# Layer 0's entry written in another order: modulation steps beside turning products, ctx's squares among x's, single PSUM banks, ropes behind the values

## The chip, the cores and the metric

One core of one Trainium2 chip runs the whole program: two transformer blocks on 512 tokens (x) with a prefix of 256 context tokens (ctx), model width 1024, all in float32 accuracy. The metric is the device time of one execution in microseconds (us); lower is better.

TensorE does the matrix products in "three-pass" form: each float32 operand is split into a rounded high part and a low part (what the rounding left), and three matmuls are added in PSUM (high x high, high x low, low x high). ScalarE (ACT in the profile) makes the high parts, VectorE (DVE) or GpSimd (POOL) the low parts.

## The reference

Only the first mixer of layer 0 matters here, up to its queries, keys and values:

```python
def rmsnorm(x, g):
    y = x * lax.rsqrt(jnp.mean(x * x, axis=-1, keepdims=True) + EPS)
    return y * g
def modulate(x, g, shift, scale):
    return rmsnorm(x, g) * (1 + scale) + shift
mod  = silu(c)     @ ada_w[0] + ada_b[0]      # six parts of 1024: shift, scale, gate, ...
modc = silu(c_ctx) @ ada_w[0] + ada_b[0]
a  = modulate(h,  norm1_g[0], sh1,  sc1)      # x,   512 tokens
ac = modulate(hc, norm1_g[0], csh1, csc1)     # ctx, 256 tokens
u, v, q, k, vv = split(a @ w_in)              # q and k: 512 wide each, vv: 512 wide
q = apply_rope(q, cos, sin); k = apply_rope(k, cos, sin)
kc, vvc = split(ac @ w_in[:, KV_START:])
```

Then come a differential attention over x and ctx, a gated chunk MLP, the output product, a feed-forward part, and layer 1.

## The kernel before, in words

Activations lie with the model width on the 128 partitions: x is eight tiles `hx[k]` (128 x 512), ctx eight tiles `hc[k]` (128 x 256). Everything that the change touches is in `even()`, before the attention. The program is written as straight code. Most steps go through `run(key, ...)` (also as `act`, `dve`, `chain`, `fetch`), which keeps the order in which they are written, engine by engine; steps that do not go through it are placed by a scheduler, which goes by the written order and its own estimate of when a step can start. The engines' queues are in order: an instruction that waits holds everything behind it on its engine.

The stages of the entry, in the times of the profile:

- 8 to 44 us: the scale part of the modulation is made in four quarters. `quarter_steps(q)` runs 32 small matmuls on a slab of `ada_w` (1 MB, loaded on SP's queue) into the one bank of `fill()`; ScalarE copies the row out (`half_row`), `quarter_turn` turns it onto the partitions by a matmul, `quarter_mod` adds bias and gain (VectorE). Then `x_hi(k)`, `x_lo(k)` split x times its scale, and `project(k)` multiplies it with the k-th slice `W[k]` of 4 x 128 columns of q and k weights, adding into four accumulators `accx`. The norm's root is taken out of the product: it is multiplied in at the end. `square(...)` sums x's squares meanwhile: a ScalarE square and a VectorE addition for each k.
- `sums` adds those squares over the partitions (matmuls with ones), takes the root by a chain of ten small VectorE steps (`rsqrt_small`, Newton) and puts it on four diagonal tiles; `spread` turns that into rows (a matmul with ones). rxs and rcs are the rows of x and of ctx.
- 38 to 40 us and 50 to 52 us: `half_steps(0)`, `half_steps(1)`: the shift part, in two halves of 64 small matmuls, turned by `half_turn` and added by `shift_mod`.
- 45 to 62 us: ctx's products with the same eight `W[k]`, 258 columns (256 tokens and two columns with the shift of x and of ctx, whose products are the biases `bc`) into `accc`. `sums(rcs)` stands ahead of k = 4, `spread` ahead of k = 7. `c_hi`, `c_lo` split ctx's operand.
- 62 to 113 us: `ada_four` (part of the later modulation, 16 matmul groups, into `fill()`), then the values: eight k, each one unit of the v weights against six 128-token tiles. The operand `AX_[k]` is made for each k by `normed` (times root and scale) and `shifted` (plus shift, split). Among these steps stand, for every second k, the steps on q and k: times rxs, plus bias, ctx's part times rcs, ScalarE's bias on ctx's part. `rope` follows: a VectorE shuffle into a `tmp("t")` tile (two buffers), a VectorE product with cos, and two GpSimd steps. After k = 4 `ada_four` runs again, ScalarE copies its row into a `tmp("t")` tile (line 465), and after k = 5 `ada_out` turns that row on TensorE.

PSUM has eight banks: three of `bank()`, one of `fill()`, and a pool of four more. Before, the entry uses them as two tiles of two banks (`wide()`), with two accumulators in each.

## Time and profile before

| | |
|---|---|
| median of 3 runs | 1539.58 us (1539.14 to 1540.97) |
| the profiled execution | 1540.77 us, of which 1539.0 us lie between its first and last instruction (the span) |
| mean granted clock of TensorE | 0.993 |
| busy share of the span | TensorE 97%, VectorE 71%, GpSimd 53%, ScalarE 48% |
| moved by DMA | 162.27 MB, 105 GB/s on average |
| TensorE busy from 10 to 100 us | 81.7 of 90 us |

The profile's views used here: the page's first part (busy time), the waits (who waited for whom), the timeline (one instruction a line: start, duration, engine, line of the code, tiles written <- read, sizes, and in brackets the idle time before it and what ended it), and windows (busy time of each engine in a stretch, with the granted clock as a share of full speed). TensorE's matmuls overlap: a 128x512 one is listed with some 0.39 us, but in a run of them one starts every 0.23 us, and a 128x258 one every 0.12 us; what a stage takes is read from starts.

### The profile page before, as it was taken

How to read it: one execution, taken by the hardware profiler on the slowest of the kernel's cores; microseconds unless marked ns; L12 is line 12 of the kernel's file. 1: busy time of each engine (PE TensorE's matmuls, PEld its weight loads, DVE VectorE, ACT ScalarE, POOL GpSimd, SP SyncE). 2: the span in 40 equal slices, each digit the busy share in tenths (PEclk: the TensorE clock that was granted, in tenths of full speed). 3: DMA queues.
4: the chain of work that ended last, by engine and by line, in shares of the span. 5: the costliest groups of instructions: out<-in, count | busy, mean ns of one | idle time of the engine just before them, and what ended most of it. 6: DMA issues, size and time to landing. Idle time of an engine off the chain costs nothing.

```text
span 1539.0 us, 25035 instructions
## 1 busy us (share of the span) xinstructions
PE 1494.3 (97%) x9573; PEld 1345.9 (87%) x9573; DVE 1091.6 (71%) x1941; ACT 738.6 (48%) x1518; POOL 818.7 (53%) x557
## 2 busy tenths in 40 slices
PE   9989999899999999999999999999999999999998
PEld 7758888799999999999999988777879899999997
DVE  4862887766788788888786487676667976666655
ACT  4434666554543333333333354667665554444444
POOL 2352330051266776677776544541323498888882
PEclk9999999999999999999999999999999999999999
DMA  9853100051132332444542211210134232323201
GB/s 353 322 195 126 46 7 1 30 191 54 69 109 98 130 113 101 144 166 143 171 166 75 81 42 57 68 42 15 62 117 165 68 111 97 110 92 115 89 22 56
DMA packets 54504, 162.27 MB, mean 105 GB/s; under 512 B 6256, under 2 KB 8688, under 8 KB 46704
## 3 DMA queue, kind: packets, MB, share of 16 engines
q1 hardware_dynamic: 47328, 135.37, 25.3%
q10 hardware_dynamic: 7056, 25.30, 4.8%
q8 instruction: 75, 1.23, 0.3%
q14 instruction: 45, 0.37, 0.1%
HBM read 158.55 MB, written 2.10 MB: 104 GB/s over the span
## 4 chain that ended last, share of the span: by engine, by line
PE 77%; DVE 11%; ACT 3%; issue 2%; POOL 1%; DMA 0%; DVEq 0%; ACTq 0%; POOLq 0%
PE pw L116 10%; PE pw L115 10%; PE pw L117 10%; PE pb L115 8%; PE pb L116 8%; PE pb L117 8%; PE pf L115 3%; PE pf L116 3%; PE pf L117 3%; PE pb L1943 3%; PE pb L1932 2%; PE pw L1894 1%; DVE t L49 1%; PE pw L1897 1%; PE pf L49 1%
## 5 line engine op out<-in xcount | busy, mean ns | idle before, releaser
L1092 DVE SCALAR_TENSOR_TENSOR xT<-pb,mod,xT 128x512 f32<-128x512 f32 (+3 forms) x204 | 143.2, 708 | 128.4 <-PE pb L117 128.2
L116 PE MATMUL pw<-ax,w 128*128 128x384 f32 (+2 forms) x716 | 227.2, 318 | 3.1 <-DVE ax L49 3.0
L115 PE MATMUL pw<-ax,w 128*128 128x384 f32 (+2 forms) x716 | 226.6, 318 | 3.3 <-DVE q L49 1.9
L117 PE MATMUL pw<-ax,w 128*128 128x384 f32 (+2 forms) x716 | 226.7, 317 | 0.1
L49 POOL TENSOR_TENSOR w<-raw,w 128x512 fp32r<-128x512 f32 x122 | 185.6, 1539 | 47.4 <-ACT w L49 47.2
L92 POOL TENSOR_TENSOR w<-raw,w 128x512 fp32r<-128x512 f32 (+1 forms) x70 | 102.1, 1465 | 197.3 <-ACT w L89 167.1
L49 POOL TENSOR_TENSOR w<-t,w 128x512 fp32r<-128x512 f32 x99 | 149.6, 1515 | 55.6 <-ACT w L49 55.6
L115 PE MATMUL pb<-hh,w 128*128 128x512 f32 x480 | 171.0, 356 | 1.2 <-DVE xT L1092 1.2
L117 PE MATMUL pb<-hh,w 128*128 128x512 f32 x480 | 171.5, 357 | 0.4 <-DVE w L49 0.4
L116 PE MATMUL pb<-hh,w 128*128 128x512 f32 x480 | 171.1, 356 | 0.0
L115 PE MATMUL pw<-T,w 128*128 128x384 f32 (+1 forms) x508 | 156.6, 310 | 2.5 <-DVE hs L1300 1.2
L116 PE MATMUL pw<-T,w 128*128 128x384 f32 (+1 forms) x508 | 157.0, 310 | 1.2 <-DVE T L132 1.2
L117 PE MATMUL pw<-T,w 128*128 128x384 f32 (+1 forms) x508 | 157.0, 310 | 0.0
L115 PE MATMUL pf<-ax,w 128*128 128x256 f32 (+2 forms) x444 | 146.8, 331 | 1.2 <-ACT f L828 0.7
L117 PE MATMUL pf<-ax,w 128*128 128x256 f32 (+2 forms) x444 | 145.7, 328 | 0.0
L116 PE MATMUL pf<-ax,w 128*128 128x256 f32 (+2 forms) x444 | 144.7, 326 | 0.0
L116 PEld LDWEIGHTS pw<-ax,w 128*128 128x128 f32 x716 | 135.9, 190 | 8.4 <-DVE ax L49 4.5
L115 PEld LDWEIGHTS pw<-ax,w 128*128 128x128 f32 x716 | 135.4, 190 | 8.3 <-DVE q L49 2.6
L117 PEld LDWEIGHTS pw<-ax,w 128*128 128x128 f32 x716 | 135.8, 190 | 2.5 <-DVE w L1263 0.4
L49 POOL TENSOR_TENSOR hh<-hs,hh 128x768 fp32r<-128x768 f32 (+1 forms) x42 | 77.9, 1855 | 93.0 <-ACT hh L49 68.8
L49 POOL TENSOR_TENSOR w<-rawo,w 128x512 fp32r<-128x512 f32 x59 | 103.6, 1757 | 28.2 <-ACT w L49 28.2
L240 DVE SCALAR_TENSOR_TENSOR junk<-ar,cb 128x1024 bf16<-128x1024 f32 x64 | 106.8, 1669 | 0.0
(445 smaller groups left out, 3925.0 us busy)
## 6 DMA issues: line engine op xcount, KB each, us to landing
raw<-ffn_in SPq DMA_DIRECT2D x44, 1024.0 KB, 5.4
ar<-ada ACTq DMA_DIRECT2D x48, 512.0 KB, 3.5
rawo<-ffn_out SPq DMA_DIRECT2D x88, 256.0 KB, 2.9
ar<-ada SPq DMA_DIRECT2D x20, 1024.0 KB, 8.4
raw<-odd_out SPq DMA_DIRECT2D x28, 256.0 KB, 2.6
ar<-adas SPq DMA_DIRECT2D x8, 512.0 KB, 7.4
raw<-qk SPq DMA_DIRECT2D x16, 256.0 KB, 5.2
raw<-uv SPq DMA_DIRECT2D x16, 256.0 KB, 2.7
```

The source lines that it names most:

```text
L49: self.tail[key] = fn(*args, **kw)
L92: eng.tensor_tensor(lo, raw, hi.bitcast(F32), ALU.subtract)
L115: mm(out, s[0], m[0], start=start, stop=False, **kw)
L116: mm(out, s[0], m[1], start=False, stop=False, **kw)
L117: return mm(out, s[1], m[0], start=False, stop=stop, **kw)
L240: return self.nc.vector.scalar_tensor_tensor(junk, t, 1.0, self.cb[who], ALU.mult, ALU.mult, accum_out=self.acc[who][:, col:col + 1])
L1092: ins = self.nc.vector.scalar_tensor_tensor(h, ps[:, r], self.modcol(l, j, m, who), h, ALU.mult, ALU.add)
L1894: nc.tensor.matmul(ps[:, st:en], Q, K[g][p][:, b0 * P:b1 * P], start=p == 0, stop=p == 1, skip_group_check=True)
L1897: last = nc.tensor.matmul(ps[:, en:en + TC], Q, K[g][p][:, TX:], start=p == 0 and not edge, stop=p == 1, skip_group_check=True)
L1932: last = nc.tensor.transpose(pt[:, x * P:(x + 1) * P], es[2 * (x % 2) + x // 2][:, kb * P:(kb + 1) * P], self.ident)
L1943: nc.tensor.matmul(po[64 * h:64 * h + 64, :], V[vb][:, 64 * g:64 * g + 64], t[:, h * TC:h * TC + TC], start=kb == 0, stop=kb == nb - 1, sk ...
```

## The change

Nothing is computed otherwise; all of it is order and place. In the words of the code:

1. Loads: the slab of quarters 1 to 3 is fetched ahead of its pair of `W` slices, not behind it.
2. Modulation: `quarter_steps(3)` and `half_steps(0)` move into the middle of `project(3)` and `project(5)`, right behind the turn; `half_steps(1)` from ctx's k = 3 to right behind `project(7)`.
3. `sums` is cut in two. The matmuls over x's squares go into the middle of `project(7)`; the root (`rooted`) follows after the evictions of `accx`, and x's `spread` moves from ahead of ctx's products to ctx's k = 2.
4. ctx's squares 0 to 3 move ahead of `project(7)`, squares 4 to 7 ahead of ctx's products; `c_hi`, `c_lo` of k = 6, 7 go behind `half_steps(1)`'s turn. `sums(rcs)` stays at k = 4; its `spread` moves from k = 7 to k = 6.
5. The accumulators are four tiles of one bank (`single()`); the pool is given back and opened again ahead of the attention. The row of `ada_four` is copied into a `tmp("q")` tile.
6. All steps on q and k and the four ropes move behind the values' code. The bias steps lose their fixed order.

```diff
-        idle = self.wide()
+        idle = self.single()
@@ ada_four
-                row = self.tmp("t")
+                row = self.tmp("q")
                 nc.scalar.copy(row, ps_of.pop(j))
@@ loads
         for k in range(2, KT, 2):
+            slabs[k // 2] = quarter_load(k // 2)
             w_load(k)
             w_load(k + 1)
-            slabs[k // 2] = quarter_load(k // 2)
             x_load(k)
@@
         def sums(acc, T):
-            rd = self.rstd_diag([(acc, T)], 1.0 / D)[0]
-            self.tail["PE"], self.tail["DVE"] = self.last_sum, self.last_diag
-            return rd
+            ps = self.bank()
+            for j in range(T // P):
+                c = slice(j * P, (j + 1) * P)
+                chain(nc.tensor.matmul, ps[:, c], acc[:, c], self.ones, start=j == 0, stop=True, ...)
+            return ps, T // P
+
+        def rooted(ps, n):
+            ms, dg = self.small(n), self.tmp()
+            with tc.issue_after(self.tail["DVE"].ins):
+                nc.vector.tensor_scalar(ms, ps[:, :n * P]..., 1.0 / D, EPS, ALU.mult, ALU.add)
+            rt = self.rsqrt_small(ms, n)
+            for j in range(n):
+                self.tail["DVE"] = nc.vector.tensor_scalar(dg[:, j * P:(j + 1) * P], self.ident, rt[:, j:j + 1], None, ALU.mult)
+            return dg[:, :n * P]
@@ x's products
+        row = quarter_steps(1)
         for q in (1, 2, 3):
             k = 2 * q
-            row = quarter_steps(q)
             got = []
-            project(k - 1, lambda: got.append(quarter_turn(row)))
+            def mid():
+                got.append(quarter_turn(row))
+                if q > 1:
+                    got.append(quarter_steps(3) if q == 2 else half_row(half_steps(0)))
+            project(k - 1, mid)
...
             project(k)
+            row = got[1] if q > 1 else quarter_steps(2)
...
-        row = half_steps(0)
-        with tc.issue_after(self.tail["PE"].ins), tc.issue_after(self.tail["DVE"].ins):
-            rd = sums(rxs, TX)
-        project(7, lambda: got.append(half_turn(row)))
+        c_squares(0, 4)
+        def mid():
+            got.append(half_turn(row))
+            with tc.issue_after(self.tail["PE"].ins):
+                got.append(sums(rxs, TX))
+        project(7, mid)
+        last = half_steps(1)
...
-        rx = spread(rd)
-        act(nc.scalar.copy, rxs, rx)
-        for i in range(2, 8):
-            c_hi(i)
-            c_lo(i)
-        w2 = [self.wide(), self.wide()]
-        accc = [w[:, h * 512:h * 512 + TC + 2] for w in w2 for h in range(2)]
+        rd = rooted(*got[3])
+        c_parts(2, 3)
+        row = half_row(last)
+        c_parts(3, 6)
+        c_squares(4, 8)
+        accc = [self.single()[:, :TC + 2] for _ in range(4)]
         for k in range(KT):
-            if k == 3:
-                row = half_steps(1)
+            if k == 2:
+                pt = half_turn(row)
+                rx = spread(rd)
+                act(nc.scalar.copy, rxs, rx)
+                shift_mod(1, pt)
+                c_parts(6, 8)
             elif k == 4:
-                with tc.issue_after(self.tail["PE"].ins), tc.issue_after(self.tail["DVE"].ins):
-                    rd = sums(rcs, TC)
-            elif k == 7:
+                ms = sums(rcs, TC)
+                rd = rooted(*ms)
+            elif k == 6:
                 rc = spread(rd)
...
@@ the operands of the values: steps on q and k taken out
-            if k % 2:
-                t = qk[keys[k // 2]]
-                dve(nc.vector.tensor_tensor, t[:, :TX], t[:, :TX], rxs, ALU.mult)
-                dve(nc.vector.tensor_scalar, t[:, :TX], t[:, :TX], bc[:, k // 2, 0:1], None, ALU.add)
-                if k // 2 % 2:
-                    dve(nc.vector.tensor_tensor, t[:, TX:], t[:, TX:], rcs, ALU.mult)
-                act(nc.scalar.activation, t[:, TX:], t[:, TX:], AF.Identity, bias=bc[:, k // 2, 1:2])
-        for n in (0, 4, 1, 5):
-            self.rope(qk[n][:, :TX], qk[n][:, :TX], tabs)
@@ behind the values
+        for n in (0, 2, 1, 3):
+            t = qk[keys[n]]
+            dve(nc.vector.tensor_tensor, t[:, :TX], t[:, :TX], rxs, ALU.mult)
+            nc.vector.tensor_scalar(t[:, :TX], t[:, :TX], bc[:, n, 0:1], None, ALU.add)
+            if n % 2:
+                dve(nc.vector.tensor_tensor, t[:, TX:], t[:, TX:], rcs, ALU.mult)
+            nc.scalar.activation(t[:, TX:], t[:, TX:], AF.Identity, bias=bc[:, n, 1:2])
+            self.rope(t[:, :TX], t[:, :TX], tabs)
@@ ahead of the attention
+        self.wp.release()
+        self.open_wide()
```

What that does to the instructions' order is shown at three places. In the rows, pb, pf and pw are PSUM tiles, ax the split operands, f the q and k tiles (f_44 to f_47 before, f_46 to f_49 after), sq the sums of squares, cp ctx's split operand, sm small columns of the root.

VectorE at the end of x's products, before:

```order
L49 TENSOR_TENSOR sq_204<-sq_204,q_457 128x512
L49 SCALAR_TENSOR_TENSOR cp<-hc_38_161,mod_70,cp 128x256 x2
L174 TENSOR_SCALAR sm_499<-pb_500 128x4
L144 TENSOR_SCALAR sm_506<-sm_499 128x4
L146 TENSOR_TENSOR sm_507<-sm_506 128x4
```

And after:

```order
L49 TENSOR_TENSOR sq_206<-sq_206,q_494 128x512
L49 SCALAR_TENSOR_TENSOR cp<-hc_38_161,mod_70,cp 128x256 x2
L49 TENSOR_TENSOR sq_206<-sq_206,q_502 128x256
L49 TENSOR_TENSOR sq_206<-sq_206,t_505 128x256
L49 TENSOR_TENSOR sq_206<-sq_206,q_508 128x256
L49 TENSOR_SCALAR f_48_202<-pw_197 128x512
L49 TENSOR_TENSOR mod_69<-pb_517,adab 128x4
L49 TENSOR_TENSOR mod_70<-pb_517,adab 128x4
L49 TENSOR_TENSOR cp<-mod_69,cp 128x4
L49 TENSOR_TENSOR cp<-mod_70,cp 128x4
L49 TENSOR_SCALAR f_47_201<-pw_198 128x512
L517 TENSOR_SCALAR sm_573<-pb_519 128x4
```

Three additions of ctx's squares and the evictions now stand ahead of x's root, which before came first.

ScalarE in the values' stage, around the copy of `ada_four`'s row (L465), before:

```order
L49 ACTIVATE ax_124<-hx_35_155,mod_69 128x512
L89 CAST w_1152<-raw_1150 128x512
L49 ACTIVATE ax_124<-hc_39_163,mod_70 128x256
L89 CAST w_1210<-raw_1208 128x512
L49 ACTIVATE f_47_201<-f_47_201,bc 128x256
L465 COPY t_1010<-pf_854 128x512
L89 CAST w_1215<-raw_1213 128x512
```

And after:

```order
L49 ACTIVATE ax_124<-hc_39_163,mod_70 128x256
L89 CAST w_1153<-raw_1151 128x512
L766 ACTIVATE f_48_202<-f_48_202,bc 128x256
L766 ACTIVATE f_49_203<-f_49_203,bc 128x256
L89 CAST w_1158<-raw_1156 128x512
L89 CAST w_1216<-raw_1214 128x512
L465 COPY q_982<-pf_826 128x512
```

The copy still stands behind the last of the steps that add a bias to q's and k's ctx part.

VectorE in the same stage, from the operands of k = 6 on, before:

```order
L49 SCALAR_TENSOR_TENSOR ax_123<-hx_35_155,mod_69,ax_122 128x512
L263 STREAM_SHUFFLE t_831<-f_45_199 128x512
L263 STREAM_SHUFFLE t_836<-f_46_200 128x512
L49 SCALAR_TENSOR_TENSOR ax_123<-hc_39_163,mod_70,ax_122 128x256
L49 SCALAR_TENSOR_TENSOR hc_39_163<-hc_39_163,mod_70,sq_204 128x256
L49 SCALAR_TENSOR_TENSOR ax_125<-hx_35_155,mod_69,ax_124 128x512
L264 TENSOR_TENSOR f_45_199<-f_45_199,cos 128x512
L264 TENSOR_TENSOR f_46_200<-f_46_200,cos 128x512
L49 SCALAR_TENSOR_TENSOR ax_125<-hc_39_163,mod_70,ax_124 128x256
L49 TENSOR_TENSOR f_47_201<-f_47_201,sq_204 128x512
L49 TENSOR_SCALAR f_47_201<-f_47_201,bc 128x512
L49 TENSOR_TENSOR f_47_201<-f_47_201,sq_204 128x256
```

And after:

```order
L49 SCALAR_TENSOR_TENSOR ax_125<-hc_39_163,mod_70,ax_124 128x256
L49 TENSOR_TENSOR f_46_200<-f_46_200,sq_206 128x512
L49 TENSOR_TENSOR f_47_201<-f_47_201,sq_206 128x512
L49 TENSOR_TENSOR f_48_202<-f_48_202,sq_206 128x512
L49 TENSOR_TENSOR f_48_202<-f_48_202,sq_206 128x256
L49 TENSOR_TENSOR f_49_203<-f_49_203,sq_206 128x512
L49 TENSOR_TENSOR f_49_203<-f_49_203,sq_206 128x256
L763 TENSOR_SCALAR f_46_200<-f_46_200,bc 128x512
L763 TENSOR_SCALAR f_47_201<-f_47_201,bc 128x512
L763 TENSOR_SCALAR f_48_202<-f_48_202,bc 128x512
L763 TENSOR_SCALAR f_49_203<-f_49_203,bc 128x512
L263 STREAM_SHUFFLE t_1095<-f_46_200 128x512
```

All operands of the values now come first, then q's and k's roots and biases, then the ropes; the reading of `ada_out`'s bank (line 412) follows behind the ropes in both.

From the start of the attention the instructions are the same, but the scheduler places some of heads 1 to 3 otherwise: of some 8,675 rows of TensorE about the 335 from row 1,015 on stand in another order, and the corresponding steps of VectorE and ScalarE with them. Behind that nothing differs.

## The prediction

> **What bounds the kernel now.** I read the page's busy times first, then who waits in the first 230 us, then the timeline at the two longest waits.

> ```profile
> span 1539.0 us, 25035 instructions
> PE 1494.3 (97%) x9573; PEld 1345.9 (87%) x9573; DVE 1091.6 (71%) x1941; ACT 738.6 (48%) x1518; POOL 818.7 (53%) x557
> ...
> PE pf L49 <- ACT t L465: 5.0, 1, 5.0
> ...
> PE pw L116 <- DVE ax L49: 1.1, 4, 0.3
> ...
> PE pb L49 <- DVE q L185: 1.0, 2, 0.7
> ```

> TensorE is the bound: only 45 us of the span are idle on it, and a change of order can win nothing else. The lines of waits (waiter <- releaser: us, times, longest) show for the entry one wait of 5.0 and small ones for x's low parts (ax) and the two spreads (q L185).

> The long wait, engine by engine (columns as in the section above):

> ```profile
> 94.15 0.39 PE L117 MATMUL pw<-w,ax 128*128 128x512 f32 x1
> 99.51 1.12 PE L49 MATMUL pf<-ident,t 128*128 128x128 f32 x4 [4.97 <-ACT t L465]
> ...
> 102.91 0.39 PE L115 MATMUL pw<-w,ax 128*128 128x512 f32 x1
> ...
> 97.97 0.41 DVE L49 TENSOR_TENSOR f<-f,sq 128x256 f32<-128x256 f32 x1
> ...
> 107.17 1.37 DVE L132 TENSOR_TENSOR vlo<-pb,vhi 128x512 fp32r<-128x512 f32 x2 [6.25 <-ACT vhi L131]
> ...
> 98.48 0.51 ACT L49 ACTIVATE f<-f,bc 128x256 f32<-128x256 f32 x1 [6.79 <-DVE f L49]
> 98.89 0.57 ACT L465 COPY t<-pf 128x512 f32<-128x512 f32 x1
> ...
> 101.00:102.00 1.00, 1.00 (x4) 0.81 (x3) 0.00 (x0) 0.00 (x0) 1.00 (x1) 0.50 1.02 426
> ```

> The row that TensorE wants to turn was complete one k of values (18 matmuls at 0.23, 4 us) ahead of 94.15. Its copy stood in ScalarE's queue behind the last bias step of q and k, and that behind VectorE, which was still at ropes and roots until 97.97. After the wait the granted clock is 0.50 (the figure ahead of the DMA share) for some 3 us. From 94.15 to 102.91 pass 8.76 us; at the pace before, four turns and seven matmuls take 0.3 + 0.4 + 1.5 = 2.2. So this place costs 6.5 us, 1.5 of them by the clock.

> **The values' stage (edits 5 and 6).** With q's and k's steps behind the operands, VectorE reaches the last step that the copy waits for without the four biases, three shuffles and three products with cos that stood ahead of it: ten instructions of 128x512 at up to 0.68 (43.91 below), up to 6.8, and without the time that GpSimd's six rope steps held it, between 0 and 1.05 each (below). So the point moves from 98 to between 85 and 91. The row is ready near 91 and wanted near 96. The copy's new tile has no rope as an earlier user. Gain 6.5.

> What is late next: the ropes end VectorE's queue there, with the reading of `ada_out`'s bank behind them, and TensorE wants that bank for the third `ada_four`, two k (8.2) and the turns after 96, at 105. Before, VectorE had done all of this at 101 (107.17 less its 6.25 of idleness); the work is the same, so I take nothing. GpSimd's weights for the next stage queue behind the ropes, wanted only after that `ada_four`.

> **The entry up to the values (edits 1 to 4).**

> ```profile
> 35.16 0.50 PE L116 MATMUL pw<-ax,w 128*128 128x512 f32 x1 [0.28 <-DVE ax L49]
> 37.87 1.95 PE L49 MATMUL pf<-ar,cst 128*32 128x128 f32 x64
> 44.15 1.10 PE L49 MATMUL pb<-q,ones 128*128 128x512 f32 x2 [0.32 <-DVE q L185]
> 54.69 0.68 PE L165 MATMUL pb<-ones,sq 128*128 128x128 f32 x4 [0.89 <-DVE mod L49]
> 60.35 0.67 PE L49 MATMUL pb<-q,ones 128*128 128x256 f32 x2 [0.65 <-DVE q L185]
> 62.40 3.64 PE L49 MATMUL pf<-ar,cst 128*32 128x512 f32 x32
> 65.97 0.50 PE L115 MATMUL pb<-w,ax 128*128 128x512 f32 x1
> ...
> 34.35 1.42 DVE L49 SCALAR_TENSOR_TENSOR ax<-hx,mod,ax 128x512 fp32r<-128x512 f32 x2 [0.40 <-ACT ax L49]
> 36.47 0.69 DVE L49 TENSOR_TENSOR sq<-sq,t 128x512 f32<-128x512 f32 x1
> 40.95 0.16 DVE L174 TENSOR_SCALAR sm<-pb 128x4 f32<-128x4 f32 x1 [2.20 <-PE pb L165]
> 43.91 0.68 DVE L49 TENSOR_SCALAR f<-pw 128x512 f32<-128x512 f32 x1
> 46.40 2.48 DVE L49 SCALAR_TENSOR_TENSOR cp<-hc,mod,cp 128x256 fp32r<-128x256 f32 x6 [0.19 <-ACT cp L49]
> 50.07 0.42 DVE L49 TENSOR_TENSOR sq<-sq,q 128x256 f32<-128x256 f32 x1
> 50.60 1.46 DVE L49 TENSOR_TENSOR sq<-sq,t 128x256 f32<-128x256 f32 x1
> 55.41 0.16 DVE L174 TENSOR_SCALAR sm<-pb 128x2 f32<-128x2 f32 x1 [0.27 <-PE pb L165]
> 55.61 1.24 DVE L144 TENSOR_SCALAR sm<-sm 128x2 int32<-128x2 int32 x1
> 60.12 2.71 DVE L49 SCALAR_TENSOR_TENSOR hx<-hx,mod,pb 128x512 f32<-128x512 f32 x4
> ...
> 50.49 2.71 POOL L92 TENSOR_TENSOR w<-raw,w 128x512 fp32r<-128x512 f32 x2 [19.38 <-DVE sq L49]
> 55.54 1.28 POOL L92 TENSOR_TENSOR w<-raw,w 128x512 fp32r<-128x512 f32 x1 [2.33 <-ACT w L89]
> ```

> TensorE's side wins. The longer middles cover two of the four waits like that of 35.16: quarter 2's whole (0.4 with the restart); quarter 3's in part, since the copy of the half's row stands ahead of `x_hi(6)` on ScalarE (0.2). x's spread no longer waits for its root (0.5): it comes behind `half_steps(1)` and two k. One bank for each accumulator takes 0.3 from the start of ctx's products, and ctx's sums wait some 0.4 less. Matmuls that move (quarters, halves, sums) cost TensorE the same at the new place. ctx's k = 6 began at 58.1 (60.35 less its wait and 12 products at 0.12); with 1.8 won TensorE is there at 56.3.

> But now ctx's spread stands at this place, and it comes from VectorE, which by these rows has no pause from x's last low parts to the end of ctx's root. I add up its queue in the new order. `x_lo(6)`: the half's steps (1.9) and their copy (0.5 with its handovers) come first, of which 0.7 lay beside quarter 3's own steps, and 0.4 were won at quarter 2: 34.35 + 1.3 = 35.7. Two low parts 1.4, three additions for x at 0.8 (0.69 and a pause like the 0.1 between 50.07 and 50.60), two ctx parts 0.85 (2.48 for six), three ctx additions at 0.53, two evictions and the shift's columns 2.0 (the 2.5 from 43.91 to 46.40 without their waits): 43.9. x's root, 40.95 to 43.91, 3.0, with 0.3 of overlap: 46.6. Four ctx parts 1.65, four additions 2.1, the second shift's columns 0.8, two parts 0.85: 52.0. ctx's root, 55.41 to 60.12, was 4.7, two of its steps held beside GpSimd splits (1.24 like that at 55.61, where its neighbours take 0.16): 2.55 without: 54.6. GpSimd splits four v slices in this stretch, as before, and each holds VectorE some 1.05 (1.46 against 0.42): 58.8. With 0.5 for handovers with ScalarE at the shift: 59.3, against 60.1 before.

> So the spread is at 59.5 instead of 60.35, and TensorE has waited 3.2 for it, not 0.65. Behind it stand two k of ctx, not one: 62.40 - 60.35 = 2.05, plus 1.45. `ada_four` starts at 63.0 and the values at 66.5: 0.5 later than 65.97. The operands of k = 0 come 5 us after VectorE's root, as before, and are no limit.

> Then the clock. The nearest rows for such a wait:

> ```profile
> 234.09 0.39 PE L115 MATMUL pb<-ath,vhi 128*128 128x256 f32 x1 [2.10 <-ACT ath L131]
> ...
> 236.00:237.00 1.00, 1.00 (x5) 0.80 (x4) 1.00 (x4) 0.02 (x1) 0.00 (x0) 0.50 0.00 0
> ...
> 210.00:220.00 10.00, 8.78 (x65) 8.00 (x64) 9.65 (x15) 7.75 (x16) 3.46 (x3) 1.00 0.00 0
> 200.00:310.00 110.00, 100.49 (x631) 88.19 (x630) 81.58 (x173) 66.89 (x138) 13.59 (x10) 0.97 0.05 18
> ```

> After a wait of 2.10 the clock was halved two microseconds later; with 1.2 idle in 210 to 220 it stayed at 1.00. 3.2 lies beyond the first, so I take the low clock here too, at some 1.2 lost (ends: 0, and the 1.5 above). The entry loses 0.5 + 1.2 = 1.7.

> Loads, on SP's queue: slabs go ahead of `W` slices, so the slices of k = 2, 3 land 1 MB later.

> ```profile
> 12.76 0.60 ACT L49 CAST wq<-raw 128x512 fp32r<-128x512 f32 x1
> ...
> 20.00:25.00 5.00, 4.89 (x48) 3.74 (x49) 3.25 (x4) 2.23 (x5) 3.10 (x2) 1.00 1.04 399
> ...
> 19.49 1.65 SPq L49 DMA_DIRECT2D ar<-ada x2
> ...
> ar<-ada SPq DMA_DIRECT2D x2, 1024.0 KB, 11.2
> ```

> At 399 GB/s that is 2.6 us: the cast of 12.76, which did not wait, runs by 15.4; its product comes after k = 0 and 1. Tighter is the first half's slab: its second load, issued at 20.8 and 11.2 on the way, landed at 32.0; behind one more v slice (0.26 MB, 0.7) 32.7, wanted some 2.1 ahead of `x_lo(6)`, at 33.6. Quarter 3's slab is wanted 5 us sooner than before and comes 0.5 MB sooner, after one fewer pair of `W` slices. I take 0, at worst 0.8; it would delay VectorE's queue with it.

> [...]

> **The attention.** It moves as a whole. Its new order in heads 1 to 3 lies where the row from 200 to 310 has 9.5 us of idle TensorE. The work is the same; a wait the more or the less is 1.2 to 3.3 us (that of 234.09 with its clock). I take 0, and 2.5 to both sides.

> **The sum.** 6.5 - 0.5 - 1.2 = 4.8 us less. The profiled execution took 1540.77 with its span of 1539.0; the median of the runs is 1539.58, 1.2 under it. The same difference off both: span 1534.2, median 1534.8. 0.2%, about what a measurement here can tell from no change, is 3.1 us.

> **The rivals.**
> 1. ctx's spread hardly waits: the third and fourth v split fall behind the root (their slots come free with ctx's k = 3 and 4, at some 52 and 55 by 56.3). Then the root ends at 57.2, the wait is 1.0, the clock stays, the values start 1.6 earlier than before: 6.5 + 1.6 = 8.1, 1531.5. Against it: before, two splits did hit the root. Chance 0.17.
> 2. The wait is there, the clock stays: 1533.6. For it: no row shows a wait of 3 us behind full work; at 234 smaller waits lay around. Chance 0.18.
> 3. The ropes hold `ada_out`'s bank. If VectorE comes to them at 93 (the late end above, 91, and four biases), and GpSimd's eight steps at 1.36 and the four cos products at 0.68 run one after another, 13.6, they end at 106.6. The point is 105; cost 1.4: 1536.2. Chance 0.10.
> 4. The change misses the copy: it still stands behind q's and k's biases on ScalarE, and if VectorE comes to them only at 98 the 6.5 stay: 1541.3. The margin is 5 us at the late end. Chance 0.05.
> 5. Slower: the attention's new order gives reordered heads one more wait each like that at 234.09, 3.3. Two give 1541.4, three 1544.7; it decides from the second on. For it: VectorE is busy 9.65 of 10 us there; against it: nothing is added. Chance 0.08.

> My forecast keeps 0.42. The range: its own is 1532.3 to 1537.3 by the attention; below it reaches past rival 1, to 1530.0, above over rival 3 with the attention's 2.5, to 1539.0. Left out are rivals 4 and 5 and a far end of rival 1. Faster by over 0.2%: rivals 1 and 2, four fifths of the forecast, half of rival 3: 0.74. Slower: half of rival 5 and a little of rival 4: 0.05. Same: 0.21.

> **What the new profile would show.** No wait of TensorE's turns for L465 and a clock of 1.00 around 100: the gain is right. ctx's spread ahead of k = 6 with a wait of 2.5 to 4, the clock at 0.5 behind it, the values' first matmul at 66.5 to 68: the loss is right; under 1.5, it is rival 1. Pauses of VectorE between 36 and 58 would show that it wasn't the limit there. A wait of the third `ada_four` for line 412 is rival 3. The whole is wrong if L465 is still waited for, or if 200 to 310 holds over 12.5 us of idle TensorE.

## The result and the profile after

| | before | changed | ratio (95% interval) |
|---|---|---|---|
| median, us | 1539.20 (14 runs) | 1535.22 (14 runs) | 0.9979 (0.9972 to 0.9986) |
| the same two, timed again | 1539.63 (26 runs) | 1537.0 (11 runs) | 0.9981 (0.9972 to 0.9991) |
| the profiled execution: time, span, mean clock | 1540.77, 1539.0, 0.993 | 1535.61, 1533.8, 0.995 | |

Of twelve executions of the changed kernel in the second row, one that took 5128.04 us is left out; the other eleven lie between 1534.20 and 1541.12.

The change is worth 4.0 us in the first row and 2.6 in the second; 1534.8 was forecast, 4.8 less. First the changed kernel's busy times from its page:

```profile
span 1533.8 us, 25030 instructions
PE 1492.7 (97%) x9573; PEld 1344.6 (88%) x9573; DVE 1089.4 (71%) x1941; ACT 738.3 (48%) x1518; POOL 817.7 (53%) x557
```

Then its waits of TensorE in the first 230 us (waiter <- releaser: us, times, longest):

```profile
PE pb L115 <- ACT ath L131: 5.5, 3, 2.3
PE pb L49 <- DVE q L521: 2.9, 1, 2.9
```

The line of 5.0 for L465 is gone; a line of 2.9 for ctx's spread (q L521) has come, and three small waits at the spreads and sums have gone. Now the place of the old wait, in the changed kernel's timeline (ScalarE, TensorE, VectorE):

```profile
92.50 0.59 ACT L465 COPY q<-pf 128x512 f32<-128x512 f32 x1 [2.94 <-PE pf L49]
...
96.58 0.60 PE L49 MATMUL pf<-ident,q 128*128 128x128 f32 x4
...
105.00 0.39 PE L117 MATMUL pw<-w,ax 128*128 128x512 f32 x1
105.32 0.64 PE L49 MATMUL pf<-ar,cst 128*32 128x512 f32 x4
...
97.22 0.26 DVE L412 TENSOR_TENSOR mod<-pf,adab 128x16 f32<-128x16 f32 x2 [0.34 <-PE pf L49]
```

And the same stretch in a window (length; busy time of PE, PEld, DVE, ACT, POOL; granted clock, DMA share, GB/s):

```profile
90.00:100.00 10.00, 10.00 (x59) 6.84 (x52) 5.89 (x10) 1.21 (x2) 10.00 (x8) 1.00 0.96 371
```

The copy runs as soon as its bank is complete (it waits for TensorE, no longer for its own queue), 4 us before its row is turned; TensorE is busy all of the window at full clock, and the third `ada_four` follows at 105.32 without a wait, its bank read at 97.22. The entry of the changed kernel, the rows for TensorE and then VectorE:

```profile
20.93 0.50 PE L115 MATMUL pw<-ax,wq 128*128 128x512 f32 x1 [0.84 <-ACT ax L49]
46.37 0.39 PE L115 MATMUL pw<-cp,w 128*128 128x258 f32 x1
59.59 0.94 PE L49 MATMUL pb<-q,ones 128*128 128x256 f32 x2 [2.87 <-DVE q L521]
64.60 3.64 PE L49 MATMUL pf<-ar,cst 128*32 128x512 f32 x32
68.17 0.50 PE L115 MATMUL pb<-w,ax 128*128 128x512 f32 x1
...
37.18 1.41 DVE L49 SCALAR_TENSOR_TENSOR ax<-hx,mod,ax 128x512 fp32r<-128x512 f32 x2 [2.08 <-ACT ax L49]
54.84 1.29 DVE L144 TENSOR_SCALAR sm<-sm 128x2 int32<-128x2 int32 x1
59.36 2.72 DVE L49 SCALAR_TENSOR_TENSOR hx<-hx,mod,pb 128x512 f32<-128x512 f32 x4
```

And the clock behind that spread, in a window (columns as above):

```profile
59.86:63.27 3.41, 3.41 (x16) 3.28 (x15) 3.27 (x6) 1.07 (x3) 0.00 (x0) 0.50 0.00 1
```

The step at 54.84 is one of ctx's root, held beside a GpSimd split (1.29, where its like takes 0.16) as the forecast had it. The values start at 68.17, just outside the 66.5 to 68 that was to show the loss and 2.20 later than the 65.97 of before, and their last matmul starts at 105.00 against 109.53: the values' stage alone won 4.53 + 2.20 = 6.73. Behind it the two profiles move apart again in steps: first product of the attention -4.55, its last -6.49, first product of the feed-forward part (hh) -6.88, last matmul -5.13. These later steps are read below.

### The profile page after: what moved, and what is told of

It reads as the page before. It is cut to its first block, busy times and chain, and to the rows that moved or that the text cites. A ratio compares the mean times of both kernels' runs of the same rounds, so it can differ in the third digit from the quotient of the medians.

```text
span 1533.8 us, 25030 instructions
## 1 busy us (share of the span) xinstructions
PE 1492.7 (97%) x9573; PEld 1344.6 (88%) x9573; DVE 1089.4 (71%) x1941; ACT 738.3 (48%) x1518; POOL 817.7 (53%) x557
## 4 chain that ended last, share of the span: by engine, by line
PE 82%; DVE 11%; ACT 3%; issue 2%; DMA 1%; POOL 0%; DVEq 0%; SPq 0%; ACTq 0%; POOLq 0%
PE pw L116 11%; PE pw L115 11%; PE pw L117 11%; PE pb L116 9%; PE pb L115 9%; PE pb L117 9%; PE pf L115 4%; PE pf L116 3%; PE pf L117 3%; PE pb L1972 3%; PE pb L1961 2%; PE pf L49 2%; PE pw L1923 1%; DVE t L49 1%; PE pw L1926 1%
## 5 line engine op out<-in xcount | busy, mean ns | idle before, releaser
L115 PE MATMUL pw<-ax,w 128*128 128x384 f32 (+2 forms) x716 | 226.6, 318 | 3.1 <-DVE q L49 1.9
L116 PE MATMUL pw<-ax,w 128*128 128x384 f32 (+2 forms) x716 | 227.1, 317 | 2.5 <-DVE ax L49 2.5
L117 PE MATMUL pw<-ax,w 128*128 128x384 f32 (+2 forms) x716 | 226.7, 317 | 0.1
L49 POOL TENSOR_TENSOR w<-raw,w 128x512 fp32r<-128x512 f32 x122 | 186.0, 1540 | 47.8 <-ACT w L49 47.6
L92 POOL TENSOR_TENSOR w<-raw,w 128x512 fp32r<-128x512 f32 (+1 forms) x70 | 102.5, 1470 | 204.3 <-ACT w L89 193.1
L49 POOL TENSOR_TENSOR w<-t,w 128x512 fp32r<-128x512 f32 x99 | 148.6, 1504 | 55.7 <-ACT w L49 55.7
L115 PE MATMUL pb<-hh,w 128*128 128x512 f32 x480 | 171.2, 357 | 2.3 <-DVE xT L1121 2.3
L117 PE MATMUL pb<-hh,w 128*128 128x512 f32 x480 | 171.8, 358 | 0.7 <-DVE w L49 0.7
L116 PE MATMUL pb<-hh,w 128*128 128x512 f32 x480 | 171.3, 357 | 0.0
L115 PE MATMUL pw<-T,w 128*128 128x384 f32 (+1 forms) x508 | 157.2, 311 | 2.5 <-DVE hs L1329 1.2
L116 PE MATMUL pw<-T,w 128*128 128x384 f32 (+1 forms) x508 | 157.4, 310 | 1.2 <-DVE T L132 1.2
L117 PE MATMUL pw<-T,w 128*128 128x384 f32 (+1 forms) x508 | 157.3, 310 | 0.0
L115 PE MATMUL pf<-ax,w 128*128 128x256 f32 (+2 forms) x444 | 146.8, 331 | 1.6 <-ACT f L857 1.1
L117 PE MATMUL pf<-ax,w 128*128 128x256 f32 (+2 forms) x444 | 144.1, 325 | 0.0
L116 PE MATMUL pf<-ax,w 128*128 128x256 f32 (+2 forms) x444 | 144.1, 325 | 0.0
L115 PEld LDWEIGHTS pw<-ax,w 128*128 128x128 f32 x716 | 135.3, 190 | 8.3 <-DVE q L49 2.6
L116 PEld LDWEIGHTS pw<-ax,w 128*128 128x128 f32 x716 | 135.9, 190 | 7.6 <-DVE ax L49 4.1
L117 PEld LDWEIGHTS pw<-ax,w 128*128 128x128 f32 x716 | 135.8, 190 | 2.5 <-DVE w L1292 0.4
L49 POOL TENSOR_TENSOR hh<-hs,hh 128x768 fp32r<-128x768 f32 (+1 forms) x42 | 78.3, 1864 | 93.4 <-ACT hh L49 68.8
L49 POOL TENSOR_TENSOR w<-rawo,w 128x512 fp32r<-128x512 f32 x59 | 103.4, 1752 | 30.1 <-ACT w L49 30.1
## 6 DMA issues: line engine op xcount, KB each, us to landing
raw<-ffn_in SPq DMA_DIRECT2D x44, 1024.0 KB, 5.2
ar<-ada SPq DMA_DIRECT2D x20, 1024.0 KB, 9.5
```

The costliest lines, as they stand in the source:

```text
L49: self.tail[key] = fn(*args, **kw)
L92: eng.tensor_tensor(lo, raw, hi.bitcast(F32), ALU.subtract)
L115: mm(out, s[0], m[0], start=start, stop=False, **kw)
L116: mm(out, s[0], m[1], start=False, stop=False, **kw)
L117: return mm(out, s[1], m[0], start=False, stop=stop, **kw)
```

## Experiments

Each is an edit of one of the two kernels. Ratios are to the kernel before.

**Edit 6 alone.** In the kernel before, as in the last but one piece of the change's diff:

```diff
-            if k % 2:
-                t = qk[keys[k // 2]]
-                ...
-        for n in (0, 4, 1, 5):
-            self.rope(qk[n][:, :TX], qk[n][:, :TX], tabs)
...
+        for n in (0, 2, 1, 3):
+            t = qk[keys[n]]
+            ...
+            self.rope(t[:, :TX], t[:, :TX], tabs)
```

> The kernel before with edit 6 alone: all steps on q and k and the four ropes stand behind the values' code; the row of ada_four still goes into a tmp("t") tile, the accumulators stay two-bank tiles, the entry keeps its old order. Theory (the copy of line 465 waited behind ScalarE's bias steps, and these behind VectorE's ropes): the entry is unchanged (values' first matmul at 66.0 +- 0.3), no wait of TensorE for line 465 is left, the clock stays at 1.00 around 100, and the values' stage alone ends some 6.5 us sooner (last values matmul at 103.0, before 109.5); the whole comes 4 to 8.5 us under the kernel before (1531 to 1535), so at or below the changed kernel. Rival A (the tile of the row, edit 5, or the new entry is needed for the gain): the wait for line 465 stays at over 3 us and the time is that of the kernel before within 1.5 us.

Median 1531.75, ratio 0.9952 (0.9940 to 0.9965). Its timeline at the copy and at the turn:

```profile
90.48 0.59 ACT L465 COPY t<-pf 128x512 f32<-128x512 f32 x1 [2.94 <-PE pf L49]
...
94.57 0.60 PE L49 MATMUL pf<-ident,t 128*128 128x128 f32 x4
```

No wait stands in the last row. The values start at 66.15 (65.97 before), and their last matmul starts at 102.99, 6.54 sooner. The theory holds to 0.2 us, and the interval lies wholly under that of the whole change: edit 6 alone is the better kernel. Run once more beside later ones:

> The kernel before with edit 6 alone once more, for a second profile and beside the two others on the same chip. Theory: the values start at 66.0 +- 0.3, no wait for line 465, the median again 2 to 5 us under the changed kernel's 1535 to 1537; the set of waits with half clock behind them differs from the first profile's (then the wait of 2.27 at the attention's first product alone), so the median lies somewhat above 1531.75 if that profile's chip drew few. Rival F (the set is fixed by the program): the same single stretch again.

Median 1533.29, ratio 0.9955 (0.9943 to 0.9967); values at 66.66, outside the 66.0 +- 0.3, since quarter 1 began 0.76 later than before. As to the clock this second profile went to rival F: again half clock at one place alone, the attention's first wait. Why that is no proof of F is shown under "the changed kernel once more".

**Its tile alone**, the tmp("q") row of edit 5 in the kernel before:

```diff
-                row = self.tmp("t")
+                row = self.tmp("q")
```

> The kernel before with one part of edit 5 alone: the row of ada_four is copied into a tmp("q") tile, not a tmp("t") tile; everything else as before. Theory (the copy stands in ScalarE's queue behind the bias steps, and the tile is not what it waits for): the wait of TensorE for line 465 stays at 4 to 5.5 us and the time is that of the kernel before within 1 us. Rival A (the copy waited because the ropes hold both tmp("t") tiles): the wait falls under 1 us, the values' stage ends some 5 to 6.5 us sooner and the whole comes 5 to 6.5 us under the kernel before.

Median 1539.80, ratio 1.0000 (0.9991 to 1.0009). The wait is there in full in its timeline:

```profile
99.61 0.51 ACT L49 ACTIVATE f<-f,bc 128x256 f32<-128x256 f32 x1 [6.79 <-DVE f L49]
100.02 0.56 ACT L465 COPY q<-pf 128x512 f32<-128x512 f32 x1
...
100.64 0.48 PE L49 MATMUL pf<-ident,q 128*128 128x128 f32 x1 [5.02 <-ACT q L465]
```

The copy stood in the queue behind the bias step, not before an occupied tile.

**The entry without edit 6.** The changed kernel with the steps on q and k among the operands again:

```diff
+            if k % 2:
+                t = qk[keys[k // 2]]
+                ...
+        for n in (0, 4, 1, 5):
+            self.rope(qk[n][:, :TX], qk[n][:, :TX], tabs)
...
-        for n in (0, 2, 1, 3):
-            t = qk[keys[n]]
-            ...
```

> The changed kernel without edit 6: the steps on q and k and the ropes stand among the values' operands again, as before; the new entry, the single banks and the tmp("q") row stay. Theory (edit 6 is the whole gain, the new entry costs): the values start at 68.2 as in the changed kernel, TensorE waits 4 to 6.5 us for line 465, and the whole is 0.5 to 4 us slower than the kernel before (1540 to 1543.5). Rival E (the new entry brings part of the gain in the values' stage): the wait for line 465 is under 3 us and the time is under that of the kernel before.

Median 1541.03, ratio 1.0012 (1.0004 to 1.0021). Its timeline:

```profile
67.87 0.50 PE L115 MATMUL pb<-w,ax 128*128 128x512 f32 x1
...
98.93 0.56 ACT L465 COPY q<-pf 128x512 f32<-128x512 f32 x1
...
99.55 0.82 PE L49 MATMUL pf<-ident,q 128*128 128x128 f32 x4 [3.11 <-ACT q L465]
```

So the new entry brings nothing here, as the theory says; the size of the wait was a miss (3.11, expected 4 to 6.5), and instructive. The copy comes at 98.93 whether the values start at 65.97 (98.89 before) or at 67.87: VectorE's queue sets it, not TensorE. The wait swallowed the entry's 1.9; the last values matmul is at 109.62 against 109.53. As long as such a wait stands, an entry that is 1.9 us later cannot be seen behind it.

**ctx's spread at k = 7 again**, in the changed kernel:

```diff
-            elif k == 6:
+            elif k == 7:
                 rc = spread(rd)
```

> The changed kernel with one part of edit 4 undone: ctx's spread stands at k = 7 again, not at k = 6. Theory (the spread at k = 6 costs TensorE its wait and, by the wait, the clock): the wait of 2.87 us falls to some 1.4 us since k = 6 of ctx now covers 1.45 us of it, the clock stays at 1.00 from 60 to 70 (0.84 in the changed kernel), the values' first matmul comes 2.0 to 2.8 us sooner (65.4 to 66.2, against 68.17), and the whole comes 1.5 to 3.5 us under the changed kernel. Rival B (the wait is the only loss, the clock falls for another reason): the values come 1.4 us sooner and the clock is still 0.5 behind 60. Rival C (the operands of the values' first k, made behind ctx's root, are the limit): the values come at 68 as in the changed kernel, with a wait just ahead of them.

Median 1533.32, ratio 0.9957 (0.9944 to 0.9969). Its timeline (TensorE, VectorE, GpSimd):

```profile
60.90 0.45 PE L49 MATMUL pb<-q,ones 128*128 128x256 f32 x1 [2.46 <-DVE q L521]
66.52 0.50 PE L115 MATMUL pb<-w,ax 128*128 128x512 f32 x1
...
59.26 1.49 DVE L521 TENSOR_SCALAR q<-ident,sm 128x128 f32<-128x128 f32 x2
...
59.21 1.26 POOL L92 TENSOR_TENSOR w<-raw,w 128x512 fp32r<-128x512 f32 x1 [1.57 <-ACT w L89]
```

The values come 1.65 sooner, where 2.0 to 2.8 were expected, the clock stays at 1.00 behind it, the whole is faster. But the wait fell to 2.46 only, not to 1.4: with k = 6's products ahead of the spread, a weight slot comes free sooner (ScalarE's cast into it runs at 58.52, where it waited for the last of those products; in the changed kernel at 63.19), GpSimd's next split starts at 59.21 instead of behind the root, and VectorE's last step of the root (two of 128x128) takes 1.49 beside it, where it takes 0.48 in the changed kernel.

**The wait filled.** In the changed kernel, matmuls of ones into the idle bank ahead of the spread; they compute nothing that is used. First 20, then 12:

```diff
+                busy = self.fill()
+                for _ in range(20):
+                    chain(nc.tensor.matmul, busy[:, :P], self.ones, self.ones, start=True, stop=True, ...)
                 rc = spread(rd)
```

> The changed kernel with 20 more matmuls of ones with ones (128x128, into the bank of fill(), read by nobody) ahead of ctx's spread at k = 6, some 2.2 to 2.7 us of work in the 2.87 us in which TensorE waits there; their results are used nowhere. Theory (the idle time itself halves the clock behind it): the spread starts at the same 59.6, the clock stays at 1.00 behind it, the values' first matmul comes 1.0 to 1.3 us sooner (66.9 to 67.2, against 68.17), and the whole comes 0.5 to 1.7 us under the changed kernel. Rival B (the low clock there has another cause than the wait): the clock is still near 0.5 from 60 to 63, the values start at 68.2 and the time is that of the changed kernel.

> The changed kernel with 12 more matmuls of ones ahead of ctx's spread at k = 6 (20 of them took 4.46 us in the run before and overshot the wait by 1.5 us; 12 take 2.68 us of the wait's 2.87). Their results are used nowhere. Theory (the wait halves the clock behind it in most executions, 4 of 4 profiles with this wait): the spread is where it was against the ctx products, no half clock from 58 to 64, and the values' first matmul comes 1.0 to 1.4 us sooner, counted from ctx's first product (20.4 to 20.8 us behind it, against 21.80); the whole 0.5 to 1.5 us under the changed kernel (1533.7 to 1535.4). Rival B (half clock there in spite of the filled wait): still 21.8 us from ctx's first product to the values.

The first gave 1536.76, ratio 0.9977 (0.9967 to 0.9987), the second 1533.39, ratio 0.9952 (0.9941 to 0.9964). The fill and the spread in the timeline with 20, and then in that with 12, where the values' first matmul stands too:

```profile
56.95 4.63 PE L49 MATMUL pf<-ones 128*128 128x128 f32 x40
61.41 0.60 PE L49 MATMUL pb<-q,ones 128*128 128x256 f32 x2
```

```profile
56.57 2.84 PE L49 MATMUL pf<-ones 128*128 128x128 f32 x24
59.60 0.67 PE L49 MATMUL pb<-q,ones 128*128 128x256 f32 x2 [0.18 <-DVE q L521]
...
66.66 0.50 PE L115 MATMUL pb<-w,ax 128*128 128x512 f32 x1
```

The clock behind the spread with 12, in a window:

```profile
61.10:64.51 3.41, 3.41 (x34) 2.38 (x36) 3.41 (x8) 1.83 (x7) 0.90 (x1) 1.00 0.00 0
```

Each float32 matmul of ones is two rows, 0.22 us together (x40 for 20, 4.46 from the first to the spread); I had costed it at half, so 20 overshot by 1.5: the clock stayed at 1.00 behind the spread, as the theory says, but the values came at 68.41, not at 66.9 to 67.2. Twelve fit: the spread starts at 59.60 as in the changed kernel (59.59), ctx's first product at 46.38 (46.37), and the values at 66.66, 1.51 sooner (1.0 to 1.4 expected). The two go alike up to the spread, so half clock behind it costs 1.51 us, where TensorE has work without a gap behind it. The whole gained more than that, 1533.39 against 1535.22 and 1537.0; not all of it is the fill's, since the scheduler placed the attention otherwise here, which is worth some 0.8 (below); the rest was not traced.

**VectorE's step on subg elsewhere.** In the changed kernel:

```diff
-        nc.vector.tensor_scalar(self.subg, self.subg, 0.8, None, ALU.mult)
+        with tc.issue_after(self.tail["DVE"].ins):
+            nc.vector.tensor_scalar(self.subg, self.subg, 0.8, None, ALU.mult)
```

> The changed kernel with one VectorE step put elsewhere: the scaling of subg (128x1), which waits for a small load that stands behind 1 MB slabs on SP's queue, comes behind the written VectorE steps instead of between the two steps of quarter 1's modulation. Theory (this step is the missed cost of the entry): quarter 1's second step comes right behind its first, project(2) starts 0.8 to 1.3 us sooner (19.6 to 20.1, against 20.93), VectorE's row of work moves with it, ctx's spread comes at 58.5 to 58.9, the values' first matmul 0.7 to 1.2 us sooner (67.0 to 67.5), with the clock halved behind the spread as often as in the changed kernel; the whole -1 us, within what the run-to-run number of half-clock stretches (1.7 us each) lets one see. Rival D (quarter 1 waits for something else, such as its slab or ScalarE): project(2) stays at 20.9 and the values at 68.2.

Median 1532.43, ratio 0.9959 (0.9946 to 0.9972). The reason is in VectorE's rows in quarter 1's modulation in the profiles of before, of the changed kernel and of this one, with the load that the step reads (SP's queue), and in the last also TensorE's spread and first values matmul:

```profile
9.34 0.35 SPq L43 DMA_DIRECT2D subg<-subln  x1
...
17.59 0.15 DVE L762 TENSOR_SCALAR subg<-subg 128x1 f32<-128x1 f32 x1 [3.83 <-DMA subg<-subln]
18.14 0.17 DVE L49 TENSOR_TENSOR pb<-pb,adab 128x2 f32<-128x2 f32 x1 [0.39 <-PE pb L49]
```

```profile
11.24 0.33 SPq L43 DMA_DIRECT2D subg<-subln  x1
...
18.63 0.17 DVE L49 TENSOR_TENSOR pb<-pb,adab 128x2 f32<-128x2 f32 x1 [4.34 <-PE pb L49]
19.90 0.15 DVE L791 TENSOR_SCALAR subg<-subg 128x1 f32<-128x1 f32 x1 [1.10 <-DMA subg<-subln]
19.97 0.15 DVE L49 SCALAR_TENSOR_TENSOR mod<-pb,gains 128x2 f32<-128x2 f32 x1
```

```profile
18.57 0.17 DVE L49 TENSOR_TENSOR pb<-pb,adab 128x2 f32<-128x2 f32 x1 [4.38 <-PE pb L49]
18.77 0.16 DVE L49 SCALAR_TENSOR_TENSOR mod<-pb,gains 128x2 f32<-128x2 f32 x1
...
58.43 0.46 PE L49 MATMUL pb<-q,ones 128*128 128x256 f32 x1 [2.86 <-DVE q L521]
67.02 0.50 PE L115 MATMUL pb<-w,ax 128*128 128x512 f32 x1
```

Before, the small load was issued at 9.34 and its step stood where VectorE was idle anyway. In the changed kernel it was issued at 11.24, behind a slab, and the step stood between the two halves of quarter 1's modulation: 1.10 of waiting for a scale that the attention wants much later. Put late, project(2) starts at 19.87 and everything up to the values 1.1 sooner, the spread too. Rival D is out. The whole came lower by more than the 1 us expected; its profile also shows the wait for xT (below) at 1.20, where the changed kernel has 2.25.

**The changed kernel once more**, unaltered.

> The changed kernel once more, unaltered, for a second profile. Theory (whether a wait of 1 to 3 us halves the clock is decided by where it falls in a time grid that runs on its own, so it differs between executions of one kernel): the waits stand at the same places with the same lengths (2.87 for ctx's spread, 2.27, 2.10, 1.34, 2.25), but the set of those with half clock behind them differs from that of the first profile in at least two places; each stretch of half clock costs 1.7 us. Rival F (the wait's length or what stands around it decides): the same waits (2.87, 1.34, 2.25, 1.14) halve the clock again and the others again do not.

Theory: right, as the set differs at three places. The first profile has half clock at four places (60, 302, 442, 1149), this one at seven (59, twice as long; 185, 304, 444, 1151, 1188, 1229), behind waits of the same lengths. All four places of the first come again, as rival F has it; that three others join them is against F. Windows of 3.41 us of the first profile, then of the second:

```profile
182.74:186.15 3.41, 2.12 (x18) 2.12 (x19) 2.84 (x8) 2.84 (x10) 0.00 (x0) 1.00 0.02 7
186.15:189.56 3.41, 3.41 (x29) 3.26 (x28) 3.09 (x9) 3.36 (x8) 0.00 (x0) 1.00 0.00 0
...
438.73:442.14 3.41, 1.16 (x6) 0.63 (x5) 3.41 (x6) 2.33 (x5) 3.41 (x3) 1.00 0.27 79
442.14:445.55 3.41, 3.41 (x14) 3.41 (x14) 2.80 (x5) 1.20 (x3) 3.41 (x3) 0.50 0.26 77
1145.29:1148.70 3.41, 1.92 (x14) 1.54 (x13) 3.41 (x7) 3.41 (x8) 3.01 (x3) 1.00 0.00 0
1148.70:1152.11 3.41, 3.41 (x18) 3.41 (x17) 3.41 (x6) 3.41 (x9) 2.83 (x3) 0.50 0.01 2
```

```profile
181.51:184.92 3.41, 0.99 (x6) 0.54 (x4) 2.88 (x7) 3.41 (x10) 0.00 (x0) 1.00 0.17 61
184.92:188.33 3.41, 3.35 (x15) 3.35 (x16) 2.31 (x6) 1.51 (x6) 0.00 (x0) 0.50 0.02 5
```

The windows are not chosen freely. In eight profiles with two or more stretches of half clock, 41 in all without the one at each program's end, every stretch begins a whole number of periods of 3.413 us behind the first of its profile, to 0.01 of a period (in the first profile of the changed kernel at 59.86, 302.20, 442.14 and 1148.70: 71, 112 and 319 periods). The phase differs between executions: behind the same spread the stretch begins 0.27 after the spread's start in the first profile (59.86, 59.59) and 0.62 ahead of it in the second (58.62, 59.24). So in these profiles the stretches begin on a grid of 3.413 us, and the grid cuts the attention's first wait of 2.27 in two in the first profile (2.12 busy in the period, full clock behind it) and not in the second (0.99 busy, half clock). Over the 13 profiles, from 20 us to 1520, of the periods at full clock with TensorE busy for less than 1.54 us, 33 of 33 were followed by half clock; of those with 1.54 to 2.0 us, 13 of 50; of the 5576 with more, none. Which waits get half clock is in part a draw, then, and two profiles of a kernel can draw alike by chance, as those of edit 6 alone did.

**Both repairs, then with the wait filled.** The subg step late and the spread at k = 7, by the diffs above; then also matmuls of ones ahead of that spread:

```diff
+                for _ in range(10):
+                    chain(nc.tensor.matmul, busy[:, :P], self.ones, self.ones, start=True, stop=True, ...)
```

> The changed kernel with both repairs: the subg step late, and ctx's spread at k = 7. Theory: project(2) at 19.6 to 20.1, the root of ctx 1 us sooner than in the changed kernel, the spread's wait at 1.2 to 2.5 us, the values' first matmul at 65.2 to 66.0, so 2.2 to 3 us sooner than 68.17; the whole 2 to 4.5 us under the changed kernel, and level with, or up to 1 us under, the kernel with edit 6 alone (1531.75), since the new entry then starts the values no later than the old one did. Rival (VectorE's row, not the spread's place, sets the values' start): values at 67 or later and no gain over the spread at k = 7 alone (1533.3).

> The changed kernel with the subg step late, ctx's spread at k = 7, and 10 matmuls of ones (2.23 us of the 2.46 us wait seen there) ahead of the spread. Theory: all three costs of the new entry are gone: project(2) at 19.7, no half clock from 57 to 63, the values' first matmul at 64.8 to 65.4 (68.17 in the changed kernel, 66.0 before); the whole 2.5 to 4 us under the changed kernel, and 0.5 to 1.5 us under the kernel with edit 6 alone, whose values start at 66.15. Rival G (what the entry gains is lost again behind it, or in half-clock stretches): the whole is level with edit 6 alone or above it.

The first gave 1535.67, ratio 0.9969 (0.9957 to 0.9981): a miss. Its values start at 66.23, not by 66.0, because the wait of 2.46 stayed, for the reason shown at k = 7, and this time half clock stood behind it (0.50 from 58.78 to 62.19). The second gave 1532.99, ratio 0.9949 (0.9935 to 0.9962), values at 64.76, in its timeline:

```profile
56.52 2.40 PE L49 MATMUL pf<-ones 128*128 128x128 f32 x20
59.15 0.67 PE L49 MATMUL pb<-q,ones 128*128 128x256 f32 x2 [0.23 <-DVE q L521]
...
64.76 0.50 PE L115 MATMUL pb<-w,ax 128*128 128x512 f32 x1
```

It starts the values 1.2 us before the kernel of before does, and 3.41 before the changed kernel. Against edit 6 alone, 1533.29 beside it, the gain is not settled: rival G stands. The mean granted clock of its runs was 0.9947, that of edit 6 alone 0.9963, and that is enough to hide a microsecond (below).

## Why the prediction was right, and where only its sum was

**The values' stage, 6.5: right.** 6.73 in the changed kernel, 6.72 in edit 6 alone (6.54 and 0.18 of later start). VectorE reached the last step that the copy waits for at 86.0 (85 to 91 forecast), the row was wanted at 96.58 (96), the third `ada_four` came at 105.32 (105) with no wait, so that rivals 3 and 4 fall. (Rival 3's cost was mis-added: 106.6 less 105 is 1.6, not 1.4.)

**The entry, -1.7: -2.20, and the spread's time right by luck.** The spread was forecast at 59.5 and came at 59.59; the wait 3.2, measured 2.87, as TensorE came at 56.72, not 56.3 (0.15 of that is a slip: 60.35 less 0.65 and 12 times 0.12 is 58.26, not 58.1); half clock behind it, as forecast. Rivals 1 and 2 did not occur. From 37.18 to 59.36 VectorE pauses for 0.24 at most at a time, so it was the limit there. But the way there was wrong at two terms. The term for the loads ("I take 0, at worst 0.8") looked at slabs and missed a 0.5 KB load and its step on VectorE, 1.1; the step's new row was there to be read in VectorE's order. So `x_lo(6)` came at 37.18, not 35.7 (0.5 of it from a later start). And VectorE's row from there to the root's end took 59.36 - 37.18 = 22.2, where I had added up 23.6: 1.4 too much, spread over small terms (0.7 up to x's root, 0.5 at ctx's four additions, 0.4 from the shift to ctx's root, 0.25 the other way at x's root) and by chance nearly what the start was too early. With the subg step away the spread is at 58.43.

**The clock, 1.2: 1.51, for another reason than I gave.** I set a limit between waits of 1.2 and 2.10. The runs show no such limit: a wait of 1.14 had half clock behind it in the first profile of the changed kernel (its period was idle for 1.49 in all), one of 2.27 had not. What half clock went with is how busy TensorE was in one period of the grid (33 of 33 under 1.54 us, 13 of 50 from there to 2.0). The wait of 2.87 (2.86 with subg late and without edit 6) had half clock behind it in all four profiles that have it (the changed kernel twice and these two); one of 2.46 had it once and once not. Idleness of 1.4 us within one period was enough once (1.98 busy ahead of the half clock at 1188 in the second profile), and 1.9 always was (33 of 33).

**The attention, 0: some 0.8 against the change, though the profiles say -1.94.** From the start of its first product to that of its last, before took 117.36 and the changed kernel 115.42. From 200 to 310 the changed kernel's TensorE is idle for 9.4 us, where 12.5 was the sign of rival 5, so that this rival falls:

```profile
200.00:310.00 110.00, 100.58 (x636) 86.73 (x635) 84.66 (x180) 66.85 (x137) 9.35 (x7) 0.98 0.06 23
```

But before had two stretches of half clock there (188 and 236), the changed kernel none, and that hides what the order does. Over the 13 profiles TensorE's rows stand in one of three orders there: that of before (also edit 6 alone, the other row tile, 12 and 10 matmuls of ones), that of the changed kernel (also 20 matmuls of ones, subg late, without edit 6), and a third with the spread at k = 7 (also both repairs). With one stretch, behind the first wait, the order of before took 116.02, 116.02 and 116.03, that of the changed kernel 116.79, 116.84 and 116.88, the third 116.06. So by these profiles the new order costs some 0.8, which the forecast had put at 0, with 2.5 to both sides; no run changed the order alone. Without any stretch the new order took 115.42 and 115.44; the old one has no such profile.

**What no term held.** At 441.94 the changed kernel waits 2.25 for xT where before waited 1.18. Over all profiles this wait is one of the two, 1.16 to 1.20 in six and 2.25 to 2.27 in seven, and the two kernels profiled twice kept theirs; GpSimd is busy through it (3.41 of 3.41 in the row above), but so it is where the wait is short (all of the 1.18 in the kernel before). What makes a kernel take the one or the other was not tried.

**The sum.** The forecast was 4.8. The entry took 0.5 more, xT 1.1 and the attention's order 0.8, and the values' stage gave 0.2 more, which makes 2.6. Measured were 4.0 and, timed again, 2.6; that the first came so near the forecast is in part luck, since xT, which had no term, and the order, which stood at 0, cost 1.9 together. The difference between the two timings lies within the draw of half clock. Over 150 runs of all kernels here, a microsecond of clock short of full speed, (1 - mean clock) x span, goes with 0.53 us of time within one kernel (straight line through each kernel's own mean, standard error 0.03), and explains 65% of the spread between runs of one kernel; the mean clocks are on record to 0.001, 1.5 us of span, so the line is rough. The means of all runs, as they ran and put to the same clock of 0.995 by that line:

| | runs | as run, us | at clock 0.995 |
|---|---|---|---|
| before | 55 | 1539.8 | 1539.1 |
| the entry without edit 6 | 11 | 1541.7 | 1539.1 |
| the whole change | 25 | 1536.5 | 1535.1 |
| edit 6 alone | 11 | 1532.8 | 1533.9 |

So edit 6 is worth 6.9 as run and 5.2 at equal clock, and the rest of the change, the attention's order with it, costs 3.6 and 1.3 where nothing hides it. Neither column is the whole truth: the second leaves out the half clock that edit 6 itself takes away (1.5 forecast behind the copy's wait) and that the new entry itself brings (1.51 behind the spread), the first holds what each kernel's runs happened to draw.

## What to carry to other kernels

Before a stage is made better, look for a wait behind it that does not move with it: as long as the copy stood behind VectorE's ropes, an entry 1.9 us later cost nothing by the end of the values' stage (109.62 against 109.53), and an earlier one would by the same reading have won nothing there, which no run tried. In a new order, read every row that came between two rows of a chain, however small: a 128x1 step that waits for a 0.5 KB load held the whole entry for 1.1 us. And fill a wait on TensorE like the 2.87 here if it cannot be removed: half clock stood behind it in four of four profiles, and cost 1.51 beside the wait itself. And where a scheduler places steps, compare the order behind the edit too: twelve matmuls of ones ahead of the spread changed it in the attention.
